# Normalizing attention probabilities in the product that transposes them

## The chip, the cores and the metric

The kernel runs on one core of one Trainium2 chip. The metric is the device time of one execution in microseconds. Five engines work side by side, each through its own queue in order: PE (TensorE: matrix products, with PEld for its loads of the stationary operand), DVE (VectorE), ACT (ScalarE), POOL (GpSimd) and SP (SyncE, which issues DMAs). They wait for one another by semaphores.

## The reference, cut to what matters

The kernel computes one layer of a decoder for 2048 prompt tokens and 64 sample tokens: a projection, sliding-window attention with learned sinks beside gated linear attention (GLA), an output projection, and a squared-ReLU MLP. The part that the change touches is the softmax of the prompt's attention:

```python
def sink_softmax(scores, mask, sink):
    scores = jnp.where(mask, scores, -jnp.inf)
    m = jnp.maximum(jnp.max(scores, axis=-1, keepdims=True), sink)
    p = jnp.exp(scores - m)
    return p / (jnp.sum(p, axis=-1, keepdims=True) + jnp.exp(sink - m))

# in swa_banded: blocks of 128 queries against 256 keys (own block and the one before)
    p = sink_softmax(scores, mask, sink)
    out = jnp.einsum('bnhgqk,bnkhd->bnqhgd', p.astype(v.dtype), vv)
```

There are 8 query heads in two groups of four, each group with one key and value head of 64 columns.

## The kernel before, in words

The prompt's attention is the kernel's first stage. It goes over 16 blocks of 128 tokens (`for i in range(NB)`, L772), and in each block over four units (`for u in range(4)`, L807). A unit (`unit`, L452) is one block, one key head `r` and two of its query heads `jj`. Its steps, each ended by a `yield` so that the loop can place it:

1. POOL copies the sink into column `nk` of the tile `s` (L460).
2. PE forms the scores of two heads in `sc`, four products of 256 columns (L465).
3. DVE adds the mask and takes the row's extreme into `m` (two instructions, L472).
4. ACT takes the exponential of scores and sink, and sums them into `den` (two instructions, L479).
5. DVE inverts `den` (L483) and multiplies each head's 256 exponentials by it (L484, two TENSOR_SCALARs).
6. PE transposes the two heads' 128x256 probabilities in four pieces of 128x128 into one PSUM bank, `pT` (L487 to L490). In block 0 there are only 128 keys and two pieces.
7. ACT copies `pT` to `ph`, rounded to the format that PE multiplies fast (fp32r, L495), and 8. DVE forms the rest `pl` = `pT` - `ph` (L497).
9. PE multiplies `ph` and `pl` by the values into `av` (L499 to L514); 10. ACT copies one half of it, 11. DVE adds the two halves into `mo` (L519).

Three units are under way at a time, called `behind`, `now` and `ahead`. The order of every engine's queue is written out by hand (L807 to L833): a pass of the loop issues the mask step of `now`, the rest `pl` of `behind`, the exponentials of `now`; then products from `fill`, the `av` products of `behind`, more fill, then four transpositions of a later block's input (`x_half`) or of the next block's rotated queries and keys (`heads_T`), more fill, the normalization of `now`, the scores of `ahead`, the transposition of `now`, and ACT's copy of it. How many fill products stand where is in `A_FILL` (L56). `fill` is the projection of later blocks to queries, keys and values, in products of 384 columns. `A_PLAN` (L58) places the rest of a block's work: scaling the projection, the rotary embedding (`rotate`, L375, on POOL, by L382 to L397), copies and rests of the transposed heads. DVE, ACT and PE are used through `InOrder` (L129), which keeps their instructions in the written order; its call (L139) is the line that the profile shows for most of them, so instructions are told apart by their tiles.

The sample tokens have units of their own (`sample_unit`, L524). After the attention come the GLA (from L872), whose output is formed by true fp32 products at L1130 to L1133, the output projection and the MLP.

Of the kernel before, what the change touches and what calls it, by code (L numbers as in the profile page):

```python
# [12 lines left out]
F32 = mybir.dt.float32  # L13
# [3 lines left out]
ALU = mybir.AluOpType  # L17
# [4 lines left out]
P = 128  # L22
# [102 lines left out]
def f32(ap):  # L125
    return ap.bitcast(F32)
# [23 lines left out]
def hybrid_step_kernel(ctx: ExitStack, tc: tile.TileContext, I, O):  # L150
# [21 lines left out]
    te, ac, dv = (InOrder(tc, engine) for engine in (nc.tensor, nc.scalar, nc.vector))  # L172

    def open_pool(name, side="left"):
        return tc.alloc_tile_pool(name=name, bufs=1, side=side, reuse_waits="tile")

    def bank(shape, kind, name):

        return ps.tile(shape, F32, tag=kind, name=name, bufs=1 if kind in "de" else 2)
# [19 lines left out]
    ident = cpool.tile([P, P], F32, name="ident")  # L199
# [81 lines left out]
    sp = open_pool("a_s")  # L281
# [170 lines left out]
    def unit(i, r, jj, mo):  # L452

        nkt = min(i + 1, 2)
        nk = nkt * P
        rr = half_of[r]
        u_ = f"{i}_{r}_{jj}"
        h0 = r * 4 + jj * 2
        s = sp.tile([P, 2, nk + 1], F32, tag="s", name=f"s_{u_}", bufs=3)
        nc.gpsimd.tensor_copy(s[:, :, nk : nk + 1], sink[:, h0 : h0 + 2].unsqueeze(2))  # L460
        yield
        qs, ks, kl = heads[i]
        kh, kl = (t[:, r].rearrange("p a k -> p (a k)")[:, 2 * P - nk :] for t in (ks, kl))
        sc = bank([P, 2, nk], "b", f"sc_{u_}")
        for u in range(2):  # L465
            j = jj * 2 + u
            te.matmul(sc[:, u, :], qs[r][:, j, :], kh, start=True, stop=False)
            te.matmul(sc[:, u, :], qs[r][:, j, :], kl, start=False, stop=True)
        yield
        m = sp.tile([P, 2], F32, tag="m", name=f"m_{u_}", bufs=3)  # L470
        for u in range(2):
            dv.tensor_tensor_reduce(  # L472
                s[:, u, :nk], sc[:, u, :], amask[:, 2 * P - nk :], scale=1.0,
                scalar=sink[:, h0 + u : h0 + u + 1], op0=ALU.add, op1=ALU.min, accum_out=m[:, u : u + 1],
            )
        yield
        den = sp.tile([P, 2], F32, tag="den", name=f"den_{u_}", bufs=3)
        for u in range(2):
            ac.activation(  # L479
                s[:, u, :], s[:, u, :], AF.Exp, scale=-1.0, bias=m[:, u : u + 1], accum_out=den[:, u : u + 1]  # L480
            )
        yield
        dv.reciprocal(den, den)  # L483
        for u in range(2):  # L484
            dv.tensor_scalar(s[:, u, :nk], s[:, u, :nk], den[:, u : u + 1], None, op0=ALU.mult)
        yield
        pT = bank([P, nkt, 2, P], "c", f"pT_{u_}")  # L487
        for u in range(2):
            for kt in range(nkt):
                te.transpose(pT[:, kt, u, :], s[:, u, kt * P : (kt + 1) * P], ident)  # L490
        yield
        ph = sp.tile([P, nkt, 2 * P], F32R, tag="ph", name=f"ph_{u_}", bufs=2)
        pl = sp.tile([P, nkt, 2 * P], F32R, tag="pl", name=f"pl_{u_}", bufs=2)
        pf = pT.rearrange("p k u q -> p k (u q)")
        ac.activation(ph, pf, AF.Copy)  # L495
        yield
        dv.tensor_tensor(pl, pf, f32(ph), op=ALU.subtract)  # L497
        yield
        av = bank([P, 2 * P], "e", f"av_{u_}")  # L499
        vs = [vals[t] for t in range(i + 1 - nkt, i + 1)]  # L500
        both, hi, lo = ([v[:, r, u] for v in vs] for u in (slice(2), 0, 1))
        both = [v.rearrange("p u d -> p (u d)") for v in both]
        out = mo[rr, jj * 2 : jj * 2 + 2].rearrange("p j q -> p (j q)")
        if nkt == 1:
            te.matmul(av[:HD], hi[0], ph[:, 0], start=True, stop=False)
            te.matmul(av[:HD], hi[0], pl[:, 0], start=False, stop=False)
            te.matmul(av[:HD], lo[0], ph[:, 0], start=False, stop=True)
            yield
            ac.activation(out, av[:HD], AF.Copy)
        else:  # L510
            te.matmul(av, both[0], ph[:, 0], start=True, stop=False)
            for kt in range(2):
                te.matmul(av[:HD], hi[kt], pl[:, kt], start=False, stop=False)
            te.matmul(av, both[1], ph[:, 1], start=False, stop=True)  # L514
            yield
            rest = sp.tile([P, 2 * P], F32, tag="spc", name=f"rest_{u_}", bufs=2)
            ac.activation(rest[:HD], av[HD:], AF.Copy)
            yield
            dv.tensor_tensor(out, av[:HD], rest[:HD], op=ALU.add)  # L519
        if (r, jj) == (1, 1):  # L520
            stores.append((mix_d[i][:, 0:4, :], mo))
        yield
# [234 lines left out]
    def units():  # L757
        for i in range(NB):
            mo = sp.tile([P, 4, P], F32, tag="mo", name=f"mo_{i}", bufs=2)
            for u in range(4):  # L760
                yield unit(i, u // 2, u % 2, mo)
        mo = sp.tile([P, 4, NS], F32, tag="mo", name="mo_s", bufs=2)
        for c in range(2):
            for r in range(2):
                yield sample_unit(c, r, cached, kcs, mo)
# [106 lines left out]
    sp = open_pool("g_s")  # L872
# [1053 lines left out]
    f, todo, slow, late = {}, deque(), deque(), DOWN_ORDER[-1]  # L1926
# [104 lines left out]
```

## Time and profile before

| | before |
|---|---|
| time, median of 3 runs (lowest to highest) | 2298.21 us (2296.2 to 2300.84) |
| profiled execution: time, span | 2298.49 us, 2296.7 us |
| PE busy, share of the span | 2214.7 us, 96% |
| PEld | 1880.2 us, 82% |
| DVE | 1611.0 us, 70% |
| ACT | 1209.7 us, 53% |
| POOL | 271.3 us, 12% |
| instructions | 34069 |

The span is the time between the first and the last event of the profiled execution; its own time has some 1.8 us more around it. Busy is the time in which at least one instruction of the engine was under way. Matmuls are pipelined, so a matmul's length holds the passage through the array, and the next one starts before it ends. A chain of waits is followed back from the last instruction, at each step to what released it. The granted clock is 1.00 at full speed. A row may hold several like instructions (x4); its length then goes from the first start to the last end.

### The profile page before, as it was taken

To read this page: it belongs to the slowest core of one execution; us is meant where nothing else is said; L and a number is where in the kernel's file an instruction comes from. 1 tells how busy PE (TensorE), PEld (TensorE's weight loads), DVE (VectorE), ACT (ScalarE), POOL (GpSimd) and SP (SyncE) were. 2 spreads that over 40 slices of the span, in tenths; PEclk is the share of its full clock that TensorE was granted. 3 is DMA by queue.
4 is the path that set the end of the run, shared out by engine and by line. 5 is a ranking of instruction groups with operands and counts; after the bars stand their busy time and mean duration, and the time that the engine had idled before them with its cause. 6 is when DMAs were issued, how large, how long until landed. Compare 5 with 4: busy or idle time off the path is not lost.

```text
span 2296.7 us, 34069 instructions
## 1 busy us (share of the span) xinstructions
PE 2214.7 (96%) x11800; PEld 1880.2 (82%) x11800; DVE 1611.0 (70%) x3345; ACT 1209.7 (53%) x2515; POOL 271.3 (12%) x428
## 2 busy tenths in 40 slices
PE   8999999999998899989999999999999999999997
PEld 7888888888887788868888878888788788888886
DVE  5888868877777766576776688787644555755557
ACT  5778755455455444455555565555444444554445
POOL 2566512111121101000000000000000000000000
PEclk9999999999999999999999999999999999999999
DMA  6343222121112355765545566666665755876665
GB/s 231 118 148 134 93 86 86 52 75 57 47 51 69 137 173 183 237 210 200 204 166 189 178 248 216 233 234 233 230 205 165 230 180 178 275 230 220 222 195 196
DMA packets 227347, 391.34 MB, mean 170 GB/s; under 512 B 23026, under 2 KB 135047, under 8 KB 223191
## 3 DMA queue, kind: packets, MB, share of 16 engines
q1 hardware_dynamic: 227174, 389.17, 50.4%
q8 instruction: 93, 1.52, 0.3%
q14 instruction: 80, 0.65, 0.1%
HBM read 254.56 MB, written 135.59 MB: 170 GB/s over the span
## 4 chain that ended last, share of the span: by engine, by line
PE 69%; DVE 16%; ACT 7%; issue 5%; DMA 2%; POOL 1%; DVEq 0%; SPq 0%; ACTq 0%; POOLq 0%
PE dn L139 24%; PE uc L139 7%; PE ua L139 7%; PE out L1243 7%; PE gproj L139 4%; PE ue L139 4%; PE ud L139 4%; PE ub L139 3%; DVE s L139 2%; PE proj L139 2%; DVE XQ L979 2%; PE sam L139 1%; PE dsam L139 1%; DVE pl L139 1%; DVE before L994 1%
## 5 line engine op out<-in xcount | busy, mean ns | idle before, releaser
L139 PE MATMUL dn<-ot,os 128*128 128x512 f32 x2688 | 623.2, 390 | 4.7 <-ACT ot L139 2.7
L139 PEld LDWEIGHTS dn<-ot,os 128*128 128x128 f32 x2688 | 504.0, 188 | 113.4 <-DVE ot L139 4.8
L139 DVE TENSOR_TENSOR os<-os 128x512 fp32r<-128x512 f32 x224 | 154.8, 691 | 229.9 <-ACT os L139 229.3
L139 ACT ACTIVATE os<-os 128x512 fp32r<-128x512 f32 x224 | 141.4, 631 | 281.3 <-DMA os<-s_d 232.1
L139 PE MATMUL gproj<-wg,gx 128*128 128x384 f32 (+1 forms) x1408 | 287.0, 350 | 0.1
L139 PEld LDWEIGHTS gproj<-wg,gx 128*128 128x128 f32 x1408 | 244.4, 190 | 13.5 <-issue 13.0
L139 ACT ACTIVATE st<-st 128x512 f32<-128x512 f32 x225 | 142.2, 632 | 140.0 <-DVE st L139 136.0
L139 PE MATMUL uc<-H,s 128*128 128x512 f32 x744 | 180.5, 392 | 4.2 <-ACT st L139 3.7
L139 PE MATMUL ua<-H,w 128*128 128x512 f32 x744 | 179.7, 390 | 0.4 <-DVE w L139 0.4
L139 PEld LDWEIGHTS uc<-H,s 128*128 128x128 f32 x744 | 140.4, 189 | 34.4 <-ACT st L139 4.1
L139 PEld LDWEIGHTS ua<-H,w 128*128 128x128 f32 x744 | 139.0, 188 | 29.2 <-DVE w L139 0.9
L215 POOL TENSOR_TENSOR frs<-rs_v,half 128x1 f32<-128x1 f32 (+1 forms) x13 | 9.2, 706 | 1263.5 <-DVE rs_v L139 1263.5
L139 DVE TENSOR_TENSOR st<-st 128x512 f32<-128x512 f32 x160 | 110.5, 692 | 66.8 <-ACT st L139 63.5
L1243 PE MATMUL out<-wo,mt 128*128 128x512 f32 x656 | 154.1, 394 | 3.3 <-DVE x L1394 3.3
L1243 PEld LDWEIGHTS out<-wo,mt 128*128 128x128 f32 x656 | 123.2, 190 | 28.7 <-issue 3.5
L139 DVE TENSOR_TENSOR ot<-ot 128x512 fp32r<-128x512 f32 x128 | 88.3, 690 | 13.9 <-ACT ot L139 13.1
L139 ACT ACTIVATE s<-t 128x1024 fp32r<-128x1024 f32 x62 | 65.8, 1061 | 60.2 <-PE ud L139 26.5
L139 PE MATMUL proj<-wa_hi,xh 128*128 128x384 f32 (+1 forms) x272 | 96.0, 356 | 0.9 <-ACT wa_hi L139 0.6
L139 PE MATMUL proj<-wa_lo,xh 128*128 128x384 f32 (+1 forms) x272 | 94.7, 352 | 0.0
L139 PE MATMUL proj<-wa_hi,xl 128*128 128x384 f32 (+1 forms) x272 | 93.5, 347 | 0.0
L139 ACT ACTIVATE ot<-ot 128x512 fp32r<-128x512 f32 x128 | 80.8, 631 | 20.5 <-DMA ot<-t_d 18.1
L139 DVE TENSOR_TENSOR s<-t,s 128x1024 fp32r<-128x1024 f32 x62 | 76.0, 1226 | 21.7 <-ACT s L139 18.4
(397 smaller groups left out, 4087.1 us busy)
## 6 DMA issues: line engine op xcount, KB each, us to landing
os<-s_d SPq DMA_DIRECT2D x224, 256.0 KB, 2.8
s_d<-st SPq DMA_DIRECT2D x31, 1792.0 KB, 10.0
raw<-in_w_up SPq DMA_DIRECT2D x64, 512.0 KB, 6.0
ot<-t_d SPq DMA_DIRECT2D x128, 256.0 KB, 3.3
rt<-in_w_down SPq DMA_DIRECT2D x96, 256.0 KB, 3.0
t<-in_w_down SPq DMA_DIRECT2D x64, 256.0 KB, 3.6
t_d<-t SPq DMA_DIRECT2D x32, 512.0 KB, 7.9
gx<-xt_d SPq DMA_DIRECT2D x28, 512.0 KB, 4.1
```

Of the source, the lines that this page charges most:

```text
L139: ins = call(*a, **k)
L215: nc.gpsimd.tensor_tensor(out, v[:n], e, op=ALU.pow)
L979: nc.vector.tensor_tensor(xq[rr, :, l, r, : n // 2].rearrange("p g (m b) -> p g m b", b=b), dr[rr], qr[rr], op=ALU.mult)
L994: nc.vector.tensor_tensor(br, br, bl[..., b - 1 :].to_broadcast(list(br.shape)), op=ALU.add)
L1243: te.matmul(p_, x, w[:, cc], start=k + u == 0, stop=k == KT - 1 and u == len(products) - 1)
```

## The change

The exponentials are no longer multiplied by the reciprocals on DVE. DVE instead builds, for each unit, a tile `dg` of two 128x128 diagonal matrices that hold the reciprocals of the two heads: the identity, read twice, times the reciprocals, each read 128 times. PE then multiplies the raw exponentials, as the stationary operand, by the head's diagonal matrix. The product is the transposed probabilities. It is a true fp32 product of the same shape as the transposition, into the same bank.

```diff
         yield
         dv.reciprocal(den, den)
-        for u in range(2):
-            dv.tensor_scalar(s[:, u, :nk], s[:, u, :nk], den[:, u : u + 1], None, op0=ALU.mult)
+        dg = sp.tile([P, 2, P], F32, tag="dg", name=f"dg_{u_}", bufs=2)
+        both = ident.unsqueeze(1).to_broadcast([P, 2, P])
+        dv.tensor_tensor(dg, both, den.unsqueeze(2).to_broadcast([P, 2, P]), op=ALU.mult)
         yield
         pT = bank([P, nkt, 2, P], "c", f"pT_{u_}")
         for u in range(2):
             for kt in range(nkt):
-                te.transpose(pT[:, kt, u, :], s[:, u, kt * P : (kt + 1) * P], ident)
+                te.matmul(pT[:, kt, u, :], s[:, u, kt * P : (kt + 1) * P], dg[:, u, :], start=True, stop=True)
```

The units of the sample tokens keep their normalization and their transpositions.

## Rows read from the trace of the kernel before

**Rows 1.** Windows of one block: us, busy of each engine, granted PE clock, DMA

```profile
150.20:167.67 17.47, 16.45 (x109) 15.21 (x109) 15.33 (x45) 13.75 (x39) 12.00 (x21) 1.00 0.37 132
```

**Rows 2.** Timeline of PE in that block: start, length, instruction, idle before

```profile
149.72 0.28 PE L139 MATMUL av<-ph,vv 128*128 128x256 f32 x1
150.20 0.45 PE L139 MATMUL av<-pl,vv 128*64 128x256 f32 x2 [0.20 <-DVE rs_v L139]
...
158.55 0.34 PE L139 MATMUL proj<-wa_lo,xh 128*128 128x384 f32 x1
159.07 0.35 PE L139 MATMUL sc<-kh,qh 128*128 128x256 f32 x1 [0.18 <-DVE qh L139]
...
159.38 0.28 PE L139 MATMUL sc<-kh,qh 128*128 128x256 f32 x1
159.50 0.28 PE L139 MATMUL sc<-kl,qh 128*128 128x256 f32 x1
159.94 0.41 PE L139 MATMUL pT<-ident,s 128*128 128x128 f32 x2 [0.16 <-ACT ql L139]
160.81 0.41 PE L139 MATMUL pT<-ident,s 128*128 128x128 f32 x2 [0.46 <-DVE s L139]
...
163.47 0.34 PE L139 MATMUL proj<-wa_lo,xh 128*128 128x384 f32 x1
163.65 0.34 PE L139 MATMUL proj<-wa_hi,xl 128*128 128x384 f32 x1
164.01 0.66 PE L139 MATMUL xT<-ident,x 128*128 128x128 f32 x4
```

**Rows 3.** Chain of waits in that block: start us, length us, engine and tile

```profile
150.22 0.55 PE av L139 x3
...
152.57 0.60 ACT ph L139
...
157.32 0.69 DVE pl L139
...
159.16 1.51 DVE s L139 x2
...
167.69 0.32 PE av L139
```

**Rows 4.** Timeline of DVE, three stretches

```profile
164.19 0.85 DVE L139 TENSOR_SCALAR s<-s,den 128x256 f32<-128x256 f32 x2
...
371.56 0.41 DVE L937 TENSOR_TENSOR ll<-zt,lh 128x256 fp32r<-128x256 f32 x1
...
395.13 1.21 DVE L937 TENSOR_TENSOR ll<-zt,lh 64x256 fp32r<-64x256 f32 x1
```

**Rows 5.** Instructions of the tile den: ns minimum, median, maximum, first and last start

```profile
L139 DVE TENSOR_SCALAR s<-s,den x128: 282/356/954, 39.7 to 314.0; 128x256 f32<-128x256 f32 x120, 128x128 f32<-128x128 f32 x8
```

**Rows 6.** Timeline of POOL, two stretches

```profile
158.78 1.73 POOL L382 TENSOR_TENSOR tb<-qk,rope 128x320 f32<-128x320 f32 x2 [0.15 <-ACT qk L139]
...
394.79 1.27 POOL L951 TENSOR_TENSOR sg<-sg,ggla 128x512 f32<-128x512 f32 x1
```

**Rows 7.** Transpositions, and fp32 products of that shape: ns minimum, median, maximum

```profile
L139 PE MATMUL pT<-ident,s x248: 270/272/303, 43.6 to 314.7; 128*128 128x128 f32 x124
...
L139 PE MATMUL o<-gp,AT x128: 272/275/275, 377.4 to 783.4; 128*128 128x128 f32 x128
```

**Rows 8.** Timeline of PE, four fp32 records and four transpositions

```profile
494.60 0.61 PE L139 MATMUL o<-gp,AT 128*128 128x128 f32 x4
495.05 0.60 PE L139 MATMUL gqk<-ident,gp 128*128 128x128 f32 x4
```

**Rows 9.** Line 1082, two inputs in SBUF: ns minimum, median, maximum

```profile
L1082 DVE TENSOR_TENSOR qd<-qk,dec x16: 425/426/946, 368.2 to 772.5; 128x256 f32<-128x256 f32 x16
```

**Rows 10.** Chain of waits, the first and the last regular block

```profile
61.19 0.55 PE av L139 x3
...
289.55 0.48 PE av L139 x4
```

## The prediction

> **What bounds the kernel now.** I read the busy times in 40 slices first, then windows of the attention stage, its chain of waits, and the PE, DVE and POOL timelines of one block. The change touches only the softmax units of the 16 prompt blocks, four units to a block; everything later keeps its instructions and is taken as shifted.
>
> One block (four units, plus the projections of a later block as fill) takes 17.47 us [rows 1]. In it PE shows 16.45 us busy, DVE 15.33, ACT 13.75, POOL 12.00: no engine has much room. PE's figure overstates its load, because the ends of short matmuls overlap the next ones, so I count PE's idle time by starts instead. Matmuls of 256 columns follow each other at 0.12 us (159.38 to 159.50), and those of 384 at 0.18 (163.47 to 163.65). Against that pace PE waits in five places [rows 2]: 149.72 to 150.20 is 0.36 too long, 158.55 to 159.07 0.34, 159.50 to 159.94 0.32, 159.94 to 160.81 (two transpositions, 0.23) 0.64, and 163.65 to 164.01 0.18. Sum 1.84 us. PE therefore needs 17.47 - 1.84 = 15.63 us of its own for a block.
>
> What makes it wait is the chain of waits [rows 3]: PE from 150.22 on, ACT from 152.57 to 157.30, DVE from 157.32 to 167.69, and PE again. The two normalizing TENSOR_SCALARs stand in it twice: 1.51 us at 159.16, and 0.85 us at 164.19 [rows 4]. Two of them undisturbed would take about 0.64 (two times the 0.356 median, overlapping a little); the longest single one is 0.954 [rows 5]. The 1.51 arise beside POOL's two rotary products, which run back to back from 158.78 to 160.51 [rows 6]: the second TENSOR_SCALAR ends 0.15 us after POOL's second product. So in this stretch the block is bound by a loop through PE, ACT and DVE, in which DVE holds 10.4 of 17.5 us and loses about 0.9 to POOL.
>
> **The change part by part.**
>
> *PE.* Each of the 248 transpositions becomes an fp32 product. The trace has 248 records for them, one each [rows 7]. It also has true fp32 products of the same shape: for the output of the gated linear attention (L1130 to L1133) the code makes 16 x 4 = 64 of them, and there are 128 records [rows 7], so an fp32 product is two records. Four records of either kind take 0.60 to 0.61 us from the first start to the last end [rows 8], with 0.27 for one: (0.61 - 0.27) / 3 = 0.113 us a record. A unit of four goes from 0.44 to about 0.88 us. A block of 16 gains 16 x 0.113 = 1.8 us (1.77 with the 0.44 of a unit), the kernel 248 x 0.113 = 28 us of PE. PE's own need for a block becomes 15.63 + 1.77 = 17.40 us, against 17.47 now: the added work nearly fills the waits, and nothing can come out below it.
>
> A rule of the Trainium skill speaks against the change: Perfetto Trace Analysis, section Transposes, wants a logical transposition done as one, since that skips the arithmetic; and TensorE: Matmul & The Clock Gate, section Terms, calls transpose mode four times faster for FP32. The first agrees with the doubled records. By the second, the sum would have three more passes of 0.113 us for each product instead of one.
>
> The rows here show a ratio of two, so I keep two records a product; four are a rival below.
>
> *DVE.* Two TENSOR_SCALARs of 128x256 go and one TENSOR_TENSOR of 128x256 comes, both inputs in SBUF. The nearest row of that shape, kind and placement takes 0.426 us at the median and 0.946 at most [rows 9]. Such an instruction is held by POOL too: the split at L937 takes 0.41 us when POOL is still, and 1.21 when it starts at 395.13 under a POOL product that began at 394.79 and lasted 1.27; it ends 0.28 us after that [rows 4, 6]. So the cost lies between 0.41 and 1.21 us; I take 0.42 where POOL is still and, in the fourth unit, the end of POOL's running product plus 0.28. That the multiplication builds a full diagonal tile out of broadcast operands changes its element count not at all. The instruction behind it in DVE's queue is the sum of the previous unit's output; the one that waits for it is PE's product, with the next unit's fill queued behind that.
>
> *ACT and the rest.* ACT's copy out of the transposition's bank reads the same tile, but 0.44 us later. Behind it in ACT's queue stand the next unit's exponentials, the square of x and the copies of q and k; in the chain ACT's stretch from 152.57 hangs on these transpositions [rows 3], so the whole ACT stretch moves by 0.44. The reciprocal stays, the exponentials keep their place, the products with V too. The new tile adds 2 KB per partition; I cost that at nothing, since the next stage's tiles are opened under PE's long run of projections.
>
> **The sum for one block.** Start at PE's 150.20, as before. Unit 1 has 0.44 more of transposition, ACT and then DVE arrive 0.44 later: the reciprocal at 159.39, the diagonal's product ready to start at 159.60. POOL's first rotary product also hangs on ACT and runs from 159.22 to 160.09 (0.87, half of the 1.73). DVE waits for it, ends at 160.09 + 0.28 = 160.37, and PE may start 0.14 later (160.66 to 160.81 is that step now), at 160.51. PE has lost the 0.34 wait at 159.07, and has 0.88 more work from two units, so it is there at 159.62 - 0.34 + 0.88 = 160.16. It waits 0.35. After that DVE is ahead: before, from the end of the TENSOR_SCALARs (160.66) to the av product (167.69) was 7.03 us; now 0.43 of it goes, and PE with 0.88 more of its own arrives last. The waits at 163.65 and at the start of the next block are gone.
>
> Block: 17.40 + 0.35 = 17.75, that is +0.28 us; counted around the loop instead (17.47 + 0.44 for unit 1, - 0.73 at the diagonal (160.66 + 0.44 - 160.37), + about 0.63 for PE's path home being longer than DVE's) it is 17.81, +0.34. I take +0.3.
>
> From 61.19 to 289.55 us there are 13 blocks of this kind [rows 10], which take 228.36 us, 1.25 more than 13 x 17.47: one of them has a further stall. 13 x 0.3 = 3.9. At the ends the cover is thinner: the first block has half the transpositions (8 x 0.113 = 0.9), and the units after 300 us have PE nearly without waits, so that some 0.44 each of three or four is exposed. I estimate +1 to +3 and take 2. Together +6. The profiled execution took 2298.49 us (span 2296.7, 1.8 around it), 0.3 above the median of the three runs, so 2298.5 + 6 = 2304.5.
>
> **Rivals.**
>
> 1. *Hidden completely.* If the diagonal's product isn't held by POOL (it would then end at 160.02, before PE's 160.16), the block is PE's own 17.40: 13 x -0.07 = -1, ends +2, about 2299.5. For it: the margin is only 0.35 us, and POOL's order may shift. Against: both POOL's product and the DVE instruction hang on the same ACT stretch, so their distance stays, and the 1.5 us of TENSOR_SCALAR now come back block after block.
>
> 2. *Faster.* DVE's relief leads and PE keeps up. The loop through DVE alone is 17.47 + 0.44 - 0.73 - 0.43 = 16.75 us, 0.7 less than now: 13 x -0.7 = -9, 2289.5. Its place is the wait before the fourth unit's transpositions; its price is PE's second pass, and it decides from PE needing no more than 16.75, that is 1.12 us more per block, 0.07 per product. At 0.09 per product the block is 17.07 and the time 2293. For it: no row shows fp32 products between the fp32r products of this stage. Against it: 0.113 a record, also for the second record of a pair.
>
> 3. *Not absorbed.* DVE's product misses the gap between POOL's two rotary products and waits out the second also: +0.87 a block, so (0.3 + 0.87) x 13 + 2 = 17, 2315.5. At the far end all 28 us are exposed, 2326.5. For it: now the second TENSOR_SCALAR does wait out the second product. Against: the first one gets in between.
>
> 4. *Four passes to one.* 16 x 3 x 0.113 = 5.4 us a block against 1.84 of waits: +3.6 on 14 blocks, about 2349. Against it stand the 128 records of 64 products; no row speaks for it. It is the factor that the Trainium skill's page TensorE: Matmul & The Clock Gate gives in its section Terms.
>
> **Chances.** Forecast 0.53, rival 1 0.25, rival 2 0.08, rival 3 0.12, rival 4 0.02. A measurement of this kernel tells some 0.2% (4.6 us) from no change. Of the forecast's own case (2301 to 2309) about a fifth lies below that, and rival 1 nearly all: slower 0.57, same 0.35, faster 0.08. The range takes rival 1 with some of rival 2's milder end, and rival 3 at its nearer end: 2295 to 2317.
>
> **What would show it.** In the profile after: 496 records for the transpositions instead of 248, at 0.11 us from start to start; 64 TENSOR_TENSORs on DVE with a mean of 0.45 to 0.6 us where 128 TENSOR_SCALARs stood; DVE some 30 us less busy in the stage; a block of 17.7 to 17.8 us between av products; PE's waits down to one, before the fourth unit's products, with POOL's rotary product ending just ahead of DVE's. Wrong would be: a block under 17.40 (then the second pass is cheaper than a record), a wait of PE elsewhere, or a difference that arises after 320 us.

## The result, and the profile after

| | before | after |
|---|---|---|
| time, median of 9 runs each, on the same chips (lowest to highest) | 2299.56 us (2296.2 to 2305.1) | 2304.54 us (2303.11 to 2308.39) |
| ratio after to before | | 1.0025, 95% interval 1.0016 to 1.0034 |
| profiled execution: time, span | 2298.49, 2296.7 us | 2306.6, 2304.8 us |

The change costs 5 us by the medians; the profiled pair is 8.1 apart. The forecast was 2304.5.

The head of the page of the kernel after (busy time, share of the span, instructions):

```profile
span 2304.8 us, 34430 instructions
...
PE 2235.2 (97%) x12048; PEld 1912.7 (83%) x12048; DVE 1592.0 (69%) x3281; ACT 1206.6 (52%) x2515; POOL 274.7 (12%) x428
```

PE is 20.5 us busier than before, DVE 19.0 less. The view of the tile dg after (count, then ns minimum, median, maximum, then first and last start); it answers to [rows 5, 7]:

```profile
L139 PE MATMUL pT<-dg,s x496: 270/275/421, 42.7 to 321.9; 128*128 128x128 f32 x166
L139 DVE TENSOR_TENSOR dg<-ident,den x64: 424/448/1036, 39.7 to 319.9; 128x256 f32<-128x256 f32 x64
```

496 records stand where 248 transpositions were, and 64 short products where 128 TENSOR_SCALARs were. One block after (the view and columns of [rows 1]; a window as long as the period, for xT starts at 153.09 and at 170.79); the period is 17.70 us against 17.47:

```profile
152.69:170.39 17.70, 17.44 (x127) 17.17 (x126) 14.05 (x40) 13.62 (x37) 12.06 (x21) 1.00 0.37 131
```

The chain of waits in that block (start us, length us, engine and tile), which answers to [rows 3]:

```profile
154.51 0.89 PE pT L139 x8
155.40 1.77 PE proj L139 x10
157.17 0.47 PE av L139 x4
157.64 0.44 PE pq L139 x4
...
158.56 0.58 ACT qh L139
...
159.65 0.61 ACT ph L139
...
160.28 0.69 DVE pl L139
...
161.20 0.69 DVE qh L139
...
162.11 0.79 DVE dg L139
162.90 0.14 issue
163.04 1.13 PE pT L139 x8
164.17 1.93 PE proj L139 x11
166.09 0.47 PE av L139 x4
```

PE now fills most of the block. A group of eight records takes 0.89 us (154.51), and the chain leaves PE only between 158.56 and 163.04, for the way to dg of the fourth unit. DVE in that stretch, and POOL beside it (timelines: start us, length us, instruction):

```profile
162.11 0.78 DVE L139 TENSOR_TENSOR dg<-ident,den 128x256 f32<-128x256 f32 x1
```

```profile
161.74 1.88 POOL L382 TENSOR_TENSOR tb<-qk,rope 128x320 f32<-128x320 f32 x2 [0.15 <-ACT qk L139]
```

The product that takes 0.42 us alone takes 0.78 under POOL's first rotary product. It is the only thing that a matmul of PE waits for in six blocks (waits of PE, 126 to 234 us: total, times, longest):

```profile
PE pT L139 <- DVE dg L139: 1.8, 7, 0.3
```

The seven waits are 1.8 / 7 = 0.26 us each by ends of records. By starts it is 0.42 in the block shown: the last sc before it starts at 162.50, the next matmul could start 0.12 later, and pT starts at 163.04.

Where the 8.1 us of the profiled pair arose, by first starts that both traces have:

| landmark | before | after | difference |
|---|---|---|---|
| first pk, first block | 49.97 | 49.52 | -0.45 |
| xT | 109.92 | 109.97 | +0.05 |
| xT, after the stalled block | 115.67 | 116.12 | +0.45 |
| pk | 120.02 | 122.52 | +2.50 |
| pk, eight regular blocks later | 259.84 | 264.07 | +4.23 |
| pk | 277.17 | 282.07 | +4.90 |
| pk of the last block | 309.96 | 316.17 | +6.21 |
| gqk, after the attention | 354.7 | 361.4 | +6.7 |
| end of the span | 2296.7 | 2304.8 | +8.1 |

The regular blocks give (4.23 - 2.50) / 8 = 0.22 us each, the last blocks, from 260 us on, another 6.21 - 4.23 = 2.0. The jump of 2.05 us between 116 and 122 us is something else, and windows show what (columns as in [rows 1]; the third number from the end is the granted clock of PE). After:

```profile
112.00:114.00 2.00, 1.70 (x10) 1.37 (x8) 0.73 (x4) 0.63 (x2) 1.93 (x4) 1.00 0.00 0
114.00:116.00 2.00, 0.67 (x4) 0.47 (x4) 0.81 (x3) 1.91 (x6) 2.00 (x3) 1.00 0.09 12
116.00:118.00 2.00, 2.00 (x14) 2.00 (x13) 1.54 (x4) 1.45 (x3) 0.37 (x1) 0.68 0.73 164
118.00:120.00 2.00, 2.00 (x11) 2.00 (x11) 1.00 (x5) 0.09 (x1) 0.05 (x1) 0.50 0.97 381
```

The same windows of the kernel before:

```profile
112.00:114.00 2.00, 1.25 (x8) 0.94 (x6) 0.92 (x5) 1.07 (x3) 2.00 (x3) 1.00 0.04 8
114.00:116.00 2.00, 1.12 (x7) 0.92 (x8) 1.22 (x5) 1.53 (x7) 1.93 (x3) 1.00 0.25 54
116.00:118.00 2.00, 2.00 (x17) 2.00 (x16) 1.78 (x7) 1.76 (x4) 0.99 (x2) 1.00 0.80 216
118.00:120.00 2.00, 2.00 (x16) 2.00 (x15) 1.80 (x8) 2.00 (x6) 0.85 (x1) 1.00 0.98 392
```

One block stalls in both kernels, where the chain runs over POOL (wg_raw) and ACT; from 112 to 116 us PE was busy for 2.37 us of 4 before (1.25 + 1.12) and after (1.70 + 0.67). After the change the granted clock then fell to its lower level (1.2 of 2.4 GHz), before it didn't. The chain after shows the price: sc takes 0.85 instead of 0.47, and eight records of pT 1.71 instead of 0.89. From 116 to 122 us the mean granted clock is 0.72, so (1 - 0.72) x 6 = 1.7 us of the 2.05 are the clock's.

```profile
112.26 1.63 POOL wg_raw L268 x2
...
114.36 0.59 ACT ph L139
...
115.73 0.55 PE av L139 x3
...
117.25 0.85 PE sc L139 x4
118.11 1.71 PE pT L139 x8
```

The clock stands behind the first landmark as well. The same window of the first block, in the kernel before, in the one after, and in the run without the rotary embedding that is described below:

```profile
36.00:54.00 18.00, 16.78 (x95) 16.36 (x95) 10.21 (x43) 9.96 (x33) 5.02 (x16) 0.81 0.44 132
36.00:54.00 18.00, 16.41 (x103) 16.14 (x104) 11.02 (x41) 10.33 (x33) 5.99 (x16) 0.91 0.51 154
36.00:54.00 18.00, 17.97 (x126) 17.64 (x125) 12.83 (x49) 12.52 (x40) 4.55 (x14) 1.00 0.67 223
```

PE of the changed kernel ran this stretch at 0.91 instead of 0.81. By an estimate that gives back (0.91 - 0.81) x 18 = 1.8 us: without it the first block would have been some 1.3 us longer than before, not 0.45 shorter.

### The profile page after: what moved, and what is told of

Same layout as the page of the kernel before. It is cut to its first block, busy times and chain, and to the rows that moved or that the text cites. A ratio compares the mean times of both kernels' runs of the same rounds, so it can differ in the third digit from the quotient of the medians.

```text
span 2304.8 us, 34430 instructions
## 1 busy us (share of the span) xinstructions
PE 2235.2 (97%) x12048; PEld 1912.7 (83%) x12048; DVE 1592.0 (69%) x3281; ACT 1206.6 (52%) x2515; POOL 274.7 (12%) x428
## 4 chain that ended last, share of the span: by engine, by line
PE 74%; DVE 12%; ACT 5%; issue 5%; DMA 2%; POOL 1%; DVEq 0%; SPq 0%; ACTq 0%; POOLq 0%
PE dn L139 23%; PE ua L139 7%; PE uc L139 7%; PE out L1244 6%; PE proj L139 4%; PE gproj L139 4%; PE ue L139 4%; PE ub L139 4%; PE ud L139 4%; PE pT L139 2%; DVE XQ L980 2%; PE sam L139 1%; PE dsam L139 1%; PE gm L139 1%; PE out L139 1%
```

## The experiments

All were timed beside the kernel before, whose medians on these chips were 2298.99 us (16 runs, with the first four kernels) and 2299.03 us (21 runs, with the other four). The theory: the added records fill PE's waits until PE itself bounds the block, and what remains is one wait, for the diagonal that POOL holds up. The rivals: the time comes from DVE's part alone, from a PE pass dearer or cheaper than a record, or from POOL's rotary product elsewhere.

**PE's part alone.** The probabilities are normalized by the TENSOR_SCALARs as before; the transposition becomes an fp32 product with the identity.

```diff
-                te.transpose(pT[:, kt, u, :], s[:, u, kt * P : (kt + 1) * P], ident)
+                te.matmul(pT[:, kt, u, :], s[:, u, kt * P : (kt + 1) * P], ident, start=True, stop=True)
```

> DVE normalizes as before; only the transpositions become fp32 products with the identity, so PE has the second records without DVE's relief. Theory (PE's second records fill PE's waits, DVE's shorter work pays for the rest): the block's loop gets 0.44 us in the second unit's transposition and the fourth unit's last two products start only after the pair of TENSOR_SCALARs, so the block goes from 17.47 to about 18.1 us; 13 x 0.63 + 2 at the ends = +10 us against before (between +7 and +13), clearly more than the changed kernel's +5. Rival (only PE's load counts, DVE's relief is worth nothing): PE's own 17.40 us a block and the same +5 us as the changed kernel.

Measured: 2311.91 us (2308.96 to 2315.64), ratio 1.0053 (1.0040 to 1.0066), +12.9 by medians. The block is 18.0 us (xT at 134.10, 152.11, 170.07). Its chain of waits:

```profile
147.17 1.53 DVE s L139 x2
148.69 0.14 issue
148.83 0.68 PE pT L139 x4
149.51 1.93 PE proj L139 x11
```

The held pair of TENSOR_SCALARs (1.53, as in [rows 3]) is still there, and PE, which before had slack behind it, has none. So the second pass costs 12.9 us without the relief, at the upper end of what was expected; the rival's +5 is out. The regular blocks hold 13 x 0.5 = 6.5 of it; the rest lies in the ends and in the stalled block, behind which this kernel's profile has the lower clock too (0.75 from 116 to 122 us).

**DVE's part alone.** The diagonal tile is built in the same place by the same kind of instruction, but with a comparison that makes it the identity, and the transposition reads it; the normalization is left out.

```diff
+        dv.tensor_tensor(dg, both, den.unsqueeze(2).to_broadcast([P, 2, P]), op=ALU.is_ge)
...
+                te.transpose(pT[:, kt, u, :], s[:, u, kt * P : (kt + 1) * P], dg[:, u, :])
```

> DVE builds a tile of the diagonal's shape with one TENSOR_TENSOR that compares instead of multiplying (it comes out as the identity), and PE transposes with it: DVE's and the waits' side of the change without the second records. The probabilities are not normalized. Theory: the loop loses 0.73 us at the fourth unit and 0.43 at the first: block about 16.3 us (15.9 to 16.8), 13 x -1.15 = -15 us against before (-9 to -18). Rival (DVE's relief is worth nothing because ACT or POOL take its place in the chain): block at 17.2 us or more, at most -4 us.

Measured: 2288.32 us (2286.13 to 2288.99), ratio 0.9948 (0.9936 to 0.9960), -10.7; the block is 16.55 (xT at 142.30, 158.84). The chain of waits shows the same held product, with one pass of PE behind it:

```profile
154.70 0.79 DVE dg L139
...
155.63 0.63 PE pT L139 x4
```

The relief is real, if less than the 15 us expected. The two parts don't add in the block: -0.92 here and +0.5 with PE's part alone would be -0.4, and both together give +0.23. With the relief alone the loop over ACT and DVE still sets the period; with both, PE is past it.

**One instruction for two, PE untouched.** The normalization of two heads in one TENSOR_TENSOR of 512 columns:

```diff
-        for u in range(2):
-            dv.tensor_scalar(s[:, u, :nk], s[:, u, :nk], den[:, u : u + 1], None, op0=ALU.mult)
+        dv.tensor_tensor(s[:, :, :nk], s[:, :, :nk], den.unsqueeze(2).to_broadcast([P, 2, nk]), op=ALU.mult)
```

> As before, but one TENSOR_TENSOR of 128x512 multiplies both heads' exponentials by their reciprocals in place of two TENSOR_SCALARs; PE transposes. Theory (two instructions can be held twice by POOL's rotary products, one only once): in the fourth unit the instruction waits out POOL's first product and takes about 0.55 us more, so the 1.51 us become about 1.05; elsewhere 0.69 against 0.64. Block 17.0 us, 13 x -0.45 = -6 us against before (-3 to -8), faster than before and than the changed kernel. Rival (the work itself, not the number of holds, is what stands in the chain): 0.69 against 0.64 a unit leaves the block at 17.4 to 17.6 us, -1 to +2 us.

Measured: 2293.57 us (2291.68 to 2296.97), ratio 0.9975 (0.9966 to 0.9984), -5.4; the block is 16.94 (xT at 148.96, 165.90). In the chain of waits the fourth unit's normalization:

```profile
157.51 1.05 DVE s L139
```

It waits out one rotary product instead of two. Where POOL is still, the one instruction is no shorter than the pair (0.69 us at 152.73 in this run, 0.62 for the pair at 154.38 before), so the wait on POOL, and not DVE's sum of work, is what the relief consists of.

**The product in the fourth unit only.** The three other units of a block keep TENSOR_SCALARs and transposition.

```diff
+        last = (r, jj) == (1, 1)
+        if last:
+            dv.tensor_tensor(dg, both, den.unsqueeze(2).to_broadcast([P, 2, P]), op=ALU.mult)
+        else:
...
+                if last:
+                    te.matmul(pT[:, kt, u, :], piece, dg[:, u, :], start=True, stop=True)
```

> Only the fourth unit of each block is normalized by the product with the diagonal; the other three keep the pair of TENSOR_SCALARs and the transposition. Theory (the gain sits in that unit's hold by POOL; the cost is 0.44 us of PE a unit): PE's own need is 15.63 + 0.44 = 16.07 us, the loop is 17.47 - 0.73 at that unit, with its longer product beside DVE's work: block 16.75 to 17.0 us, 13 x -0.6 = -8 us against before (-5 to -10). Rival (the fourth unit's longer product hands on its 0.44 us through ACT's copy to the next block): block 17.2 to 17.4 us, -1 to -4 us.

Measured: 2293.52 us (2291.84 to 2295.29), ratio 0.9973 (0.9962 to 0.9984), -5.5; the block is 17.03 (xT at 148.63, 165.66), just above the 16.75 to 17.0 that were expected; the time lies within. Its chain of waits:

```profile
157.17 0.79 DVE dg L139
...
158.09 1.13 PE pT L139 x8
...
163.09 0.69 DVE xl L139
...
164.59 0.60 DVE pl L139
```

The loop closes over DVE again (xl, pl), as before the change. The same product in the three other units turns -5.5 into +5: they add 12 x 0.113 = 1.4 us of PE a block, of which PE's waits cover a half: the block goes from 17.03 to 17.70, and 13 x 0.67 = 8.7 us. The rest of the 10.5 fits the clock: this run's profile has it at 1.00 from 112 to 122 us, where the changed kernel lost 1.7 us.

**The hold taken away.** The changed kernel without the rotary embedding of q and k (which mixes up the order of heads too), so that POOL holds nothing in the fourth unit:

```diff
+        if i > 0:
+            rots[i] = qk.rearrange("p (j r) d -> p j r d", r=2)
+            return
```

> The changed kernel without POOL's rotary products (the queries and keys stay unrotated, in another order of heads), to take away what holds DVE's product in the fourth unit. Theory (PE's own work is 17.40 to 17.45 us a block and the wait for the held product the remaining 0.25): the product takes 0.42 to 0.45 us in every unit, PE waits nowhere, block 17.4 to 17.45 instead of 17.70; 13 x -0.27 = -3.5 us against the changed kernel, so +1 to +2 us against before. Rival (PE's wait comes from ACT's and DVE's chain, the hold is an accompaniment): block stays 17.6 to 17.7 and the time at +4 to +5.

Measured: 2296.72 us (2293.10 to 2299.96), ratio 0.9989 (0.9980 to 0.9998); the block is 17.36 (xT at 141.90, 159.25, 176.61). Two windows (columns as in [rows 1]):

```profile
134.00:150.00 16.00, 16.00 (x116) 15.85 (x115) 13.13 (x39) 12.29 (x36) 6.75 (x15) 1.00 0.37 126
150.00:166.00 16.00, 16.00 (x120) 15.84 (x118) 12.78 (x39) 12.23 (x33) 6.06 (x14) 1.00 0.33 105
```

And the tile dg:

```profile
L139 DVE TENSOR_TENSOR dg<-ident,den x64: 409/425/642, 38.2 to 309.6; 128x256 f32<-128x256 f32 x64
```

PE is busy without a gap, and the chain of waits there consists of PE alone. This is the block's floor: 17.36, and 17.70 - 17.36 = 0.34 is the price of the hold. The block was as expected, the time 3 to 4 us below what was expected. Two things outside the regular blocks were missed: the first block is shorter (its pk starts at 45.89 instead of 49.52), with the granted clock at 1.00 there instead of 0.91, and behind the stalled block the clock stays at 1.00 instead of 0.72. So the time of this kernel doesn't tell the price of the hold; the block does.

**Both of the faster edits.** The product in the fourth unit, one TENSOR_TENSOR in the three others.

> The product with the diagonal in the fourth unit of each block, and one TENSOR_TENSOR for both heads in the other three, with the transposition. If the two gains lie at different places of the loop (the fourth unit's hold, the first unit's pair) they add in part: block 16.8 to 16.95 us, -6 to -9 us against before. If both only remove the same hold, it is the time of either alone, -5.5 to -6.5.

Measured: 2295.07 us (2292.14 to 2300.27), ratio 0.9985 (0.9977 to 0.9994), -4.0. This was missed in both versions of the expectation: the block is 17.07, no better than with the product alone, and the chain shows the same hold:

```profile
141.47 0.78 DVE dg L139
```

Two edits that remove one wait don't add. The regular block is that of the product alone (17.03). That the time is 1.5 us higher fits the clock, though one profile of each doesn't prove it: this one has the lower clock behind the stalled block (0.63 in 116 to 120 us), as the changed kernel's has, and the one with the product alone has 1.00.

**ACT normalizes the fourth unit.** PE keeps its transposition everywhere, DVE its TENSOR_SCALARs in three units:

```diff
+        if (r, jj) == (1, 1):
+            for u in range(2):
+                ac.activation(s[:, u, :nk], s[:, u, :nk], AF.Copy, scale=den[:, u : u + 1])
```

> As before, but in the fourth unit ACT normalizes (two copies with a scale per row, 0.4 to 0.5 us each) instead of DVE; PE transposes. ACT has 1.40 us idle before its copy of that unit's transposition and no port that POOL holds. Theory (the fourth unit's normalization is what the loop waits for): the transposition starts at about 160.3 instead of 159.9 to 160.8 and DVE has 1.5 us less, block 16.7 to 16.9 us, -7 to -10 us against before. Rival (ACT is itself in the loop, and its copy of q comes 0.9 us later): block 17.2 us or more, -3 us or less.

Measured: **2286.76 us** (2283.86 to 2289.80), ratio 0.9947 (0.9935 to 0.9960), -12.3: faster than both kernels, and by more than expected. The block is 16.59 (xT at 141.87, 158.45, 175.04). The chain of waits:

```profile
137.98 0.80 ACT s L139 x2
...
139.42 0.61 ACT ph L139
...
140.05 0.69 DVE pl L139
```

The two normalizations take 0.80 us on ACT beside POOL's product (137.46 to 139.16 in its timeline), against 1.51 on DVE [rows 3] and 0.78 for the product that then asks two passes of PE. ACT isn't held: none of the 32 normalizations on ACT takes more than 0.50 us. And PE gets no new work.

**The same, with one TENSOR_TENSOR in the three other units.**

> ACT normalizes in the fourth unit, one TENSOR_TENSOR for both heads in the other three; PE transposes. If the first unit's pair is still in the loop, it is 0.1 to 0.2 us a block better than with the pairs: block 16.6 to 16.8 us, -8 to -11 us against before. If the loop has moved to ACT, the same as with the pairs, within 1 us.

Measured: 2291.62 us (2287.76 to 2292.99), ratio 0.9962 (0.9948 to 0.9975), -7.4, outside both versions of the expectation. The block is shorter still, 16.47 (xT at 142.15, 158.62), and the chain of waits has moved to POOL:

```profile
144.40 2.02 POOL wg L270 x2
146.41 0.96 POOL rstd_all L215
...
147.40 0.59 ACT qk L139
```

Yet the kernel is slower than the one with TENSOR_SCALARs. The last pk starts at 298.0 and the first gqk at 343.3 us, against 298.2 and 343.5 in the run with TENSOR_SCALARs: level. The difference lies behind, in work that is the same in both (the last gqk 744.7 against 741.7, the first ua on w 996.0 against 988.9). In the two profiles most of it is the granted clock: 0.83 against 1.00 from 445 to 455 us, 0.83 against 1.00 from 695 to 705, and 0.87 against 0.91 from 760 to 800, together 1.7 + 1.7 + 1.6 = 5.0 of the 7.1 us. But over the five timed runs of each kernel the mean granted clock is the same, 0.990, so the 4.9 us between the medians are not explained by it; what makes them is open.

The other profiles agree with their times to within 1.7 us up to there. The first gqk starts at 354.7 us before, and at:

| kernel | first gqk | against before | time against before |
|---|---|---|---|
| after | 361.4 | +6.7 | +5.0 |
| PE's part alone | 366.9 | +12.2 | +12.9 |
| DVE's part alone | 342.4 | -12.3 | -10.7 |
| one TENSOR_TENSOR | 348.8 | -5.9 | -5.4 |
| product in the fourth unit | 349.7 | -5.0 | -5.5 |
| no rotary | 351.1 | -3.6 | -2.3 |
| product and TENSOR_TENSOR | 351.4 | -3.3 | -4.0 |
| ACT in the fourth unit | 343.5 | -11.2 | -12.3 |
| ACT and TENSOR_TENSOR | 343.3 | -11.4 | -7.4 |

## Why the prediction was right

The mechanism held: PE's second pass fills its waits, and the wait for the held diagonal remains. The value (2304.5 against 2304.54) is closer than its terms deserve, and that is luck. The forecast was +6 on 2298.5 for the kernel before; the nine runs gave +5.0 on 2299.56. The terms of the +6 err both ways too.

- *Two records a product, 0.113 us each.* Right: 496 records, eight in 0.89 us against 0.88. Four passes (rival 4) are out.
- *PE's own need of 17.40 us.* Right: 17.36 with the hold gone. The method held, to take a block's period less PE's waits counted from start to start and to add the new work. PE's busy time before, 16.45 [rows 1], plus 1.8 would have given 18.25.
- *The hold.* Right in place and price: dg ran from 162.11 to 162.89, 0.78 us where 0.77 was worked out, and cost the block 0.34 where 0.35 was said. Rival 1 (no hold) is the block of 17.36 that the run without rotary shows; rival 3 (both rotary products) didn't occur in the regular blocks, where dg of the fourth unit takes 0.76 to 0.79 us; only the one at 56.58 us, behind the first block, was held longer, 1.04 us. The Trainium skill (SBUF — State Buffer, section Who interferes with whom) states that a DVE instruction with two SBUF inputs contends with a GpSimd instruction that reads SBUF; the trace agrees, 0.78 us under POOL's product and 0.42 without.
- *Who else is late.* Partly. The chain was said to start at unit 1's transposition; it goes through PE's pq and ACT's qh instead (157.64, 158.56), with the same end.
- *The block at +0.3.* It is +0.22, so 13 blocks give 2.9 instead of 3.9 us. Both counts of the sum (+0.28, +0.34) lay above; 0.04 is PE's need.
- *The ends at +2.* The sum left the clock out. The first block became 0.45 faster, where a loss of up to 0.9 was assumed, because the clock gave back some 1.8 us there; DVE's relief alone, at 0.81 as before, has its first pk at 50.30, later than the 49.97 before. From 282 us to the first gqk 1.8 us were lost, about what was costed for that end, and 0.67 in the block before, where a regular one loses 0.22.
- *The stalled block.* Counted as a regular one, its stall as one that shifts with the rest. The profiled pair drifts 0.40 us apart over the stall itself and 2.05 behind it, 1.7 of them by the clock, for which the prediction had no term.
- *DVE 30 us less busy in the stage.* It is 19 (237.3 from 36 to 316 us before, 218.2 from 36 to 322 after, where the stage ends 6 us later). It didn't enter the time.
- *Rival 2 (faster).* Its mechanism is real: DVE's part alone gives a block of 16.55 us and -10.7. The rival's 16.75 had 0.44 for the second pass of unit 1 in it; without that its loop would be 16.31. What decided against it is the price per product, 0.113 and not under 0.07.

Not settled is how much of the 5 us of the medians belongs to the clock behind the stalled block: the profile has it, but it is one execution, and no run took the stall away. An estimate comes from the clocks that the runs show, 0.9907 in the mean of 37 runs of the kernel before (beside the experiments) and 0.9900 in the nine after: if PE needed all of it, 0.0007 x 2300 = 1.6 us. Runs of one kernel differ by more than that, 0.987 to 0.992 after.

The prediction called a difference that arises after 320 us a sign of being wrong, and the profiled pair shows one, in unchanged work: +6.7 us at the first gqk, +10.1 at the last (752.1 before, 762.3 after), +8.1 at the end. In the stretch between the two gqk the granted clock is 0.99 before and 0.98 after, and 3.4 us in 400 would need 0.008. The medians are 5.0 apart, so at least 3 of the pair's 8.1 are its own.

## What to carry to other kernels

Work added to an engine costs at least what exceeds its waits, so count those waits from start to start. It can cost more where it lengthens the loop that bounds the stage: with PE's part alone the block is 18.0 us, though PE by itself needs only the 17.36 that the run without the rotary embedding shows. So price the added and the removed part each by its own loop. Then look for the one place where the removed work was dear (here one unit in four, under POOL's rotary product) and move only that one, to an engine that POOL doesn't hold up: two ACT instructions a block in place of two TENSOR_SCALARs gave -12.3 us, the full change +5.

## What the runs showed of the hardware

- A stall of PE may cost more than its length. Behind the stalled block the granted clock stood at half for a while in five of the ten profiles (after, PE's part alone, one TENSOR_TENSOR, product and TENSOR_TENSOR, ACT and TENSOR_TENSOR), at a price of 1.7 us each; in the other five it stayed at 1.00. The length of the stall doesn't part them: PE's longest idle time there was 1.29 us after and 1.28 before, and 1.47 in DVE's part alone, where the clock stayed. What decides it is open. Where kernels differ by a few us, compare the granted clock by windows before giving the difference a cause.
- Longer DVE instructions hold POOL as well: with one TENSOR_TENSOR of 512 columns, POOL's first two rotary products took 2.14 us from start to end (1.73 before [rows 6], 1.70 beside ACT's normalization), and in that run and in the one with ACT and TENSOR_TENSOR POOL stands in the chain of waits. Its timeline, in the kernel with one TENSOR_TENSOR everywhere:

```profile
157.13 2.14 POOL L382 TENSOR_TENSOR tb<-qk,rope 128x320 f32<-128x320 f32 x2 [0.15 <-ACT qk L139]
```
